# Attention's opening and end, x loaded first, and retention scores issued later

## The chip, the core and the metric

The kernel runs on one core of a Trainium2 chip. The metric is the time of one execution in microseconds (us), the median of several runs. TensorE (PE) multiplies matrices, VectorE (DVE), ScalarE (ACT) and GpSimd (POOL) do the elementwise work, and SyncE (SP) issues the DMA transfers.

## The reference

One sequence of 512 tokens, width 1024, passes through two blocks in float32. The first has a pooling mixer layer and a dilated attention layer, each followed by a convolutional feed-forward network (FFN); the conditioning vector c gives every layer a shift, a scale and a gate. The second has two layers of retention heads and stick-breaking heads side by side, each followed by a gated FFN.

```python
def _modulate(h, shift, scale): return h * (1 + scale) + shift
mod = silu(c) @ ada_w[layer] + ada_b[layer]      # sh1, sc1, g1, sh2, sc2, g2
h = _modulate(_rmsnorm(x, norm1_g), sh1, sc1)
# layer 0: y = pool_mixer(h);  layer 1:
hkv = _modulate(_rmsnorm(x, kv_norm_g), kv_shift, kv_scale)
y = dilated_attention(h, hkv @ w_kv)             # 3 branches (dilation 1, 4, 16), 16 heads of 64
x = x + g1 * y
x = x + g2 * conv_ffn(_modulate(_rmsnorm(x, norm2_g), sh2, sc2))
# second block, per layer:
ret = chunk_retention(rotary(rq), rotary(rk), rv)  # 4 heads of 128, decayed scores
sb  = stick_breaking(sq, sk, sv)                   # 4 heads of 128
x = x + concat(group_norm(ret) * silu(rg), rms_norm(sb)) @ w_out
x = x + (silu(h @ w_gate) * (h @ w_up)) @ w_down
```

## The kernel before

Activations lie transposed, features on partitions: x is eight tiles of 128x512. Every large product is made of three passes (`mm3`, L274 to L276): the weight's rounded high part times the input's high part, times the input's low part, and the weight's low part times the input's high part. So each input h is a pair of tiles, a high and a low one. Weights come as 434 units of 128x1024 (512 KB): SP loads `raw`, ACT rounds it into `wh`, and `wl = raw - wh` is made on DVE, or on POOL for every second unit while `st["spread"]` is set (L211). There are six `raw` buffers, three each of `wh` and `wl`, and eight banks of PSUM (`ps`) that PE writes.

The order of each engine's instructions is fixed when the program is built. The large products are written as plain loops, and after each `mm3` the builder adds its cost to a modelled clock (`pe["clk"]`) and calls `pump()`. That lets three streams of generators go one step further when their `ready` time has come: a generator issues some instructions and yields the microseconds until its next step. Stream 0 carries attention cores and stick-breaking heads, stream 1 norms and retention heads, stream 2 (`ada_all`) the modulation weights, a DMA of 512 KB and one DVE product (`araw`, L140 and L365) per step, `rate[0]` apart. `need(key)` runs stream 2 on at once until a modulation vector is there.

The norm before an FFN or attention is partly hidden: PE multiplies the raw x times gain by the first weights, while the statistics (`Stat`: squares on ACT, adds on POOL and for the last few on DVE, a 128x1 product on PE at L281), the reciprocal root (`rsy`) and its broadcast R follow in `norm_gen`; R and a column of shifts correct the product afterwards, and the modulated h for the rest are made one by one.

Attention runs over four head groups and, in each, three branches. `branch_qkv` makes queries, keys and values, `branch_core` is the generator of scores, softmax (`turn` transposes the exponentials at L285) and values, `combine` mixes the branches, and `out_proj` adds a head group's share of the output to x. In a retention layer `mixer2` computes for each head the query and key products, turns them with `rotary` (three DVE steps and one POOL add, L1165), and adds `ret_head` to stream 1. Nearly all DVE and ACT instructions have line L140, a helper that keeps program order.

Of the kernel before, what the change touches and what calls it, by code (L numbers as in the profile page):

```python
# [12 lines left out]
AF = mybir.ActivationFunctionType  # L13
# [3 lines left out]
P = 128  # L17
# [109 lines left out]
def model_kernel(ctx, tc, xT, wstream, adaw, vecs, crow, tab, rope, dret, selt, bandt, outT, plan, stop=None):  # L127
    order = {"on": False}

    class Kept:  # L130
# [4 lines left out]

        def __getattr__(self, name):
            f = getattr(self.engine, name)

            def call(*a, **kw):
                r = f(*a, **kw)  # L140
                return tc.keep_in_program_order(r) if order["on"] else r

            return call

# [110 lines left out]
                self.step()  # L255

    streams = [Stream() for _ in range(3)]

    def pump():
        if pe["in"]:  # L260
# [259 lines left out]
        return h, low(t, h)  # L520

    def norm_gen(stat, specs, out, residues):
        yield 2.5 if residues else 4.5
        y = rstd(stat.mean())
        yield 2.5
        out["R"] = bcast(y, residues)
        out["h"] = [[] for _ in specs]
        if not residues:
            for m in range(KT):
                out["h"][0].append(modulate(normed(out["R"], m), *specs[0], m))  # L530
            return
        xn = [normed(out["R"], m, True) for m in range(KT)]
        for hs, spec in zip(out["h"], specs):
            for m in range(KT):
                hs.append(modulate(xn[m], *spec, m))

    class RawNorm:

# [12 lines left out]
        def finish(self):  # L551
            drain(streams[1])
            return self.out["R"], self.out["h"]

    def unraw(o, R, col):
        t = S()
        nc.vector.tensor_tensor(t, o, R, op=ALU.mult)
        nc.scalar.activation(t, t, AF.Identity, bias=col)
        return t


    def pool_mixer(g1, nx):
# [14 lines left out]
        lnexp()  # L577

# [27 lines left out]
        sh.column(1)  # L606
        R = bcast(y)
        issue_low(*wh)
        us = [[ps() for _ in range(NB)] for _ in range(2)]
# [116 lines left out]

        return ap.rearrange("p (b r i) -> p b r i", b=4, r=4)

    def branch_qkv(hg, br, h, hkv, pre=()):
        d = ORDER[br]  # L730
        col = br * D + hg * 256
        qk = [("attn_w_q", (0,), 0, col), ("attn_w_q", (0,), 0, col + P),
              ("w_kv", (), 0, col), ("w_kv", (), 0, col + P)]
        vt = []
        if d == 1:

            for j in range(2):
                o = gemm([("w_kv", (), 0, 3 * D + col + j * P)], hkv, range(KT))[0]
                t = S()
                nc.scalar.activation(blocked(t), blocks(o), AF.Copy)  # L740
                vt.append(t)
        q, k = [], []
        for i in range(4):
            if i < 2 and pre:
                q.append(pre[i])
                continue
            o = gemm([qk[i]], h if i < 2 else hkv, range(KT))[0]
            t = S()
            dst, src = (t, o) if d > 1 else (blocked(t), blocks(o))
            if i < 2:  # L750
                nc.scalar.activation(dst, src, AF.Copy, scale=0.125)
                q.append(t)
            else:
                nc.vector.tensor_copy(dst, src)
                k.append(t)
        ov = [ps(), ps()]

        def part(b):
            return ov[b // 2][:, (b % 2) * 256:(b % 2) * 256 + 256]

        if d == 1:
            for b in range(NB):
                for j in range(2):
                    tr(part(b)[:, j * P:(j + 1) * P], vt[j][:, b * P:(b + 1) * P], ident)
        else:
            for kt in range(KT):
                wH, wL = wt("w_kv", (), kt * P, 3 * D + col, n=2)
                for b in range(NB):
                    xH, xL = (a[:, b * P:(b + 1) * P] for a in hkv[kt])
                    o = part(b)  # L770
                    fl = kt == 0 and b % 2 == 0
                    nc.tensor.matmul(o, xH, wH, start=fl, stop=False, skip_group_check=True)  # L772
                    nc.tensor.matmul(o, xL, wH, start=False, stop=False, skip_group_check=True)  # L773
                    nc.tensor.matmul(o, xH, wL, start=False, stop=kt == KT - 1, skip_group_check=True)  # L774
                    pe["clk"] += 0.34
                    pump()
        v = []
# [4 lines left out]
        return q, k, v  # L782

    def branch_core(hg, br, q, k, v, parts):

        d = ORDER[br]
        st4 = smp.tile([P, NB, 8], F32, tag="st4", name=nm("st4"), bufs=8)
# [85 lines left out]
            return t  # L873

        N = []
        first = scores(0)
        yield Y[0]
        first = turn(first)
        second = scores(1)
        yield Y[10]  # L880
        N.append(values(0, first))
        yield Y[11]
        second = turn(second)
# [65 lines left out]
    def attention(nx, spec, kvspec, g1, nx2):  # L949
        done = []  # L950
        parts = []
        nx.start(kvspec, spec, residues=True)
        st["spread"] = True

        outs = [("attn_w_q", (0,), 0, br * D + j * P) for br in range(2) for j in range(2)]
        pss, cols = gemm_raw(outs, nx.raw, spec[1])
        nx.raw = None
        R, (hkv, h) = nx.finish()
        pre = []
        for j, o in enumerate(pss):  # L960
# [6 lines left out]
            nc.vector.tensor_scalar(t, t, cols[:, j:j + 1], 0.125, op0=ALU.add, op1=ALU.mult)  # L967
            pre.append(t)
        nx2 = nx2()
        stat = nx2  # L970
        for hg in range(4):
            for br in range(3):
                q, k, v = branch_qkv(hg, br, h, hkv, pre[2 * br:2 * br + 2] if hg == 0 else ())
                streams[0].add(branch_core(hg, br, q, k, v, parts))
                if br == 2:
                    streams[0].add(combine(parts, done))
        out_proj(0, done, g1, stat)
        out_proj(1, done, g1, stat)
        out_proj(2, done, g1, stat)
        drain(streams[0])  # L980
        out_proj(3, done, g1, stat)
        return nx2

    def out_proj(hg, done, g1, stat):
        while len(done) <= hg:
            pe["clk"] = max(pe["clk"], streams[0].ready)
            streams[0].step()
        g1 = g1()
        for m in range(KT):
            o = gemm([("attn_w_o", (0,), 256 * hg, m * P)], done[hg], range(2))[0]  # L990
# [3 lines left out]
            if hg == 3:  # L994
                stat.add(m)
        done[hg] = None


    def head_norm(o, center):
# [106 lines left out]
    def mixer2(l, h, fin, res, dec, cosr, sinr):  # L1106
# [151 lines left out]
    nx = attention(nx, (nx.gs, mods[(1, 0)]), (gk, mods[("kv", 0)]), mod((1, 2)), next_norm("norm2_g", 1, (1, 4)))  # L1258
    if stop == 3:
        return dump()  # L1260
    need((1, 3))
# [181 lines left out]
```

## Time and profile before

| | |
|---|---|
| median of three runs | 2711.17 us (2707.82 to 2712.11) |
| the profiled execution | 2713.44 us, span 2711.7 us |
| PE busy | 2645.2 us, 98% |
| DVE, ACT, POOL busy | 52%, 38%, 12% |
| mean granted clock of PE | 0.993 |
| HBM | 109 GB/s over the span |

Times of rows count from the start of the span. "Busy" counts an engine's own instructions; idle time in front of one is put down to what released it last. PE is busy in nearly every slice, so what an edit can win is PE's idle time and the time it runs at a lower clock, and both are to be looked for by place.

### The profile page before, as it was taken

What the parts mean: (1) busy time and instruction counts of PE and PEld (TensorE: products, weight loads), DVE (VectorE), ACT (ScalarE), POOL (GpSimd) and SP (SyncE); (2) the same over time, 40 slices, a digit from 0 to 9 for tenths busy, and PEclk for the clock granted to TensorE, in tenths of its full rate; (3) what the DMA queues carried; (4) which work ended last, traced back from release to release, by engine and by line L of the source; (5) the groups of instructions that cost most, each with busy time, mean ns of one, the idle gap of its engine ahead of it and who ended that gap; (6) DMA issues with size and microseconds to landing.
All of it is one profiled execution on the core that took longest, in us unless ns stands there. A gap on an engine that the chain in (4) does not pass through costs nothing.

```text
span 2711.7 us, 32544 instructions
## 1 busy us (share of the span) xinstructions
PE 2645.2 (98%) x12952; PEld 2184.3 (81%) x12952; DVE 1399.8 (52%) x2137; ACT 1029.9 (38%) x1720; POOL 320.0 (12%) x242
## 2 busy tenths in 40 slices
PE   6999999989999999999999999999999999999998
PEld 5878888778888888788888887888888887888887
DVE  7886566764333436753444456543434347543432
ACT  4453233544434344542344451422233451422233
POOL 0000000211221212000003011210111011110111
PEclk9999999999999999999999999999999999999999
DMA  8655555443222221222323211222233221223231
GB/s 317 230 163 179 171 178 169 144 157 116 71 77 72 78 68 66 93 101 93 101 94 117 78 62 63 93 94 101 93 101 117 80 69 47 101 93 101 94 101 47
DMA packets 86230, 297.69 MB, mean 110 GB/s; under 512 B 9574, under 2 KB 10302, under 8 KB 86078
## 3 DMA queue, kind: packets, MB, share of 16 engines
q1 hardware_dynamic: 86078, 295.61, 32.6%
q8 instruction: 101, 1.65, 0.3%
q14 instruction: 51, 0.42, 0.1%
HBM read 293.48 MB, written 2.10 MB: 109 GB/s over the span
## 4 chain that ended last, share of the span: by engine, by line
PE 61%; DVE 2%; POOL 1%; issue 0%; ACT 0%; DMA 0%; SPq 0%; DVEq 0%; POOLq 0%
PE ps L274 19%; PE ps L275 18%; PE ps L276 18%; PE ps L281 4%; DVE s L140 1%; PE ps L285 1%; POOL s L1165 0%; DVE x L140 0%; DVE wl L140 0%; ACT s L140 0%; PE ps L774 0%; PE ps L773 0%; PE ps L772 0%; PE ps L1071 0%; PE ps L1070 0%
## 5 line engine op out<-in xcount | busy, mean ns | idle before, releaser
L274 PE MATMUL ps<-s,wh 128*128 128x512 f32 x3152 | 1241.4, 395 | 0.2 <-DVE s L140 0.2
L275 PE MATMUL ps<-s,wh 128*128 128x512 f32 x3152 | 1232.2, 391 | 0.0
L276 PE MATMUL ps<-s,wl 128*128 128x512 f32 x3152 | 1230.8, 391 | 0.0
L140 ACT ACTIVATE wh<-raw 128x1024 fp32r<-128x1024 f32 x434 | 459.4, 1059 | 1024.1 <-PE ps L275 783.2
L140 DVE TENSOR_TENSOR wl<-raw,wh 128x1024 fp32r<-128x1024 f32 x394 | 492.2, 1249 | 494.5 <-ACT wh L140 482.7
L274 PEld LDWEIGHTS ps<-s,wh 128*128 128x128 f32 x3152 | 593.4, 188 | 129.6 <-issue 7.2
L276 PEld LDWEIGHTS ps<-s,wl 128*128 128x128 f32 x3152 | 593.2, 188 | 125.1 <-issue 1.1
L275 PEld LDWEIGHTS ps<-s,wh 128*128 128x128 f32 x3152 | 593.8, 188 | 119.6 <-DVE s L140 0.4
L140 ACT ACTIVATE s<-s 128x512 fp32r<-128x512 f32 (+6 forms) x288 | 167.9, 584 | 182.0 <-DVE s L140 118.6
L140 DVE TENSOR_TENSOR s<-s,s 128x512 fp32r<-128x512 f32 (+3 forms) x202 | 140.4, 698 | 75.6 <-ACT s L140 74.9
L431 POOL TENSOR_TENSOR s<-s,s 128x512 f32<-128x512 f32 x40 | 62.1, 1558 | 973.0 <-ACT s L140 972.5
L140 DVE TENSOR_TENSOR s<-ps,s 128x512 f32<-128x512 f32 (+6 forms) x164 | 103.8, 647 | 139.0 <-PE ps L276 128.8
L281 PE MATMUL ps<-s,s 128*64 128x128 f32 (+7 forms) x1376 | 156.9, 309 | 16.9 <-POOL s L1165 12.6
L140 DVE TENSOR_TENSOR s<-s,ps 128x512 f32<-128x512 f32 x108 | 73.1, 686 | 194.1 <-PE ps L276 168.2
L281 PEld LDWEIGHTS ps<-s,s 128*128 128x128 f32 (+2 forms) x1376 | 124.5, 174 | 55.3 <-issue 17.9
L211 POOL TENSOR_TENSOR wl<-raw,wh 128x1024 fp32r<-128x1024 f32 x40 | 99.8, 2494 | 414.4 <-ACT wh L140 368.5
L140 ACT ACTIVATE s<-ps 128x512 f32<-128x512 f32 (+5 forms) x188 | 97.0, 530 | 114.1 <-PE ps L281 66.9
L1198 POOL TENSOR_TENSOR s<-s,s 128x512 f32<-128x512 f32 x44 | 76.4, 1737 | 536.6 <-ACT s L140 536.6
L140 DVE COPY s<-ps 128x512 f32<-128x512 f32 (+2 forms) x73 | 48.7, 673 | 148.2 <-PE ps L285 77.1
L140 DVE SCALAR_TENSOR_TENSOR araw<-araw,cond 128x1024 f32<-128x1024 f32 x96 | 119.0, 1242 | 10.4 <-DMA araw<-in_adaw 10.4
L140 ACT ACTIVATE s<-s,st 128x128 f32<-128x128 f32 (+1 forms) x192 | 79.7, 417 | 52.3 <-DVE st L140 52.3
L140 ACT ACTIVATE s<-x 128x512 f32<-128x512 f32 x72 | 45.1, 626 | 95.2 <-DVE x L140 92.7
(117 smaller groups left out, 1770.7 us busy)
## 6 DMA issues: line engine op xcount, KB each, us to landing
raw<-in_wstream SPq DMA_DIRECT2D x434, 512.0 KB, 3.3
araw<-in_adaw SPq DMA_DIRECT2D x96, 512.0 KB, 4.3
s<-in_adaw SPq DMA_DIRECT2D x32, 256.0 KB, 6.0
x<-in_xT SPq DMA_DIRECT2D x8, 256.0 KB, 5.3
s<-in_dret SPq DMA_DIRECT2D x8, 256.0 KB, 4.5
out<-s SPq DMA_DIRECT2D x8, 256.0 KB, 2.6
s<-in_rope SPq DMA_DIRECT2D x4, 256.0 KB, 5.1
cond<-in_crow SPq DMA_DIRECT2D x1, 512.0 KB, 4.0
```

The lines of the kernel that those rows point to most:

```text
L140: r = f(*a, **kw)
L211: (nc.gpsimd if u % 2 and st["spread"] else nc.vector).tensor_tensor(l, raw, h.bitcast(F32), op=ALU.subtract)
L274: nc.tensor.matmul(out, wH, xH, start=start, stop=False, **kw)
L275: nc.tensor.matmul(out, wH, xL, start=False, stop=False, **kw)
L276: nc.tensor.matmul(out, wL, xH, start=False, stop=stop, **kw)
L281: nc.tensor.matmul(out, lhsT, rhs, start=start, stop=stop, **kw)
L285: nc.tensor.transpose(out, in_, idn)
L431: eng.tensor_tensor(self.ss, self.ss, q, op=ALU.add)
L1198: nc.gpsimd.tensor_tensor(s, s, R, op=ALU.mult)
```

## The change

- **Opening.** The eight x tiles are loaded right behind the conditioning vector. The statistics' adds stand ahead of the first modulation columns, and columns are made one step ahead instead of two.
- **Norms.** `norm_gen` first waits 8.5 (was 4.5), or 4.0 (was 2.5) for attention. In attention it makes the normalised x and the modulated keys/values input tile by tile, with a yield after each, and the queries' input after them.
- **Attention's opening.** Two value and two key outputs of the first branch run k outer, so that they take the inputs in the order in which these are made; `upto` runs the norm just as far as needed. POOL makes no low parts in head group 0. The next norm's modulation (`nx2`) is asked for at the end of attention; stream 2 starts 50 later, one step each 13.
- **Cores.** For the undilated branch the transposes of values move into the core, 2.5 later. The last core starts before its values are projected, and issues both its scores first.
- **Attention's end.** Head groups 0 and 1 share one PSUM accumulation in the output product. The statistics' adds from the third on are on DVE (`last` is 6).
- **Retention.** A head's scores wait until the modelled clock is 4.0 past the end of its key product.

```diff
+    def since(clk, us):
+        return max(0.0, clk + us - pe["clk"])
...
     def norm_gen(stat, specs, out, residues):
-        yield 2.5 if residues else 4.5
+        yield 4.0 if residues else 8.5
...
-        xn = [normed(out["R"], m, True) for m in range(KT)]
-        for hs, spec in zip(out["h"], specs):
-            for m in range(KT):
-                hs.append(modulate(xn[m], *spec, m))
+        xn = []
+        for m in range(KT):
+            xn.append(normed(out["R"], m, True))
+            out["h"][0].append(modulate(xn[m], *specs[0], m))
+            yield 2.0
+        for m in range(KT):
+            out["h"][1].append(modulate(xn[m], *specs[1], m))
+            xn[m] = None
+            yield 2.5
...
+        for m in range(KT):
+            nc.sync.dma_start(x[m], xT[m])
         nc.sync.dma_start(vec, vecs)
         nc.sync.dma_start(ident, tab[:, C_ID:C_ID + P])
         for m in range(KT):
             sc.load(m)
             sh.load(m)
-            if m == 0:
-                for i in range(KT):
-                    nc.sync.dma_start(x[i], xT[i])
...
-            if m + 2 < KT:
-                columns(m + 2)
+            if m + 1 < KT:
+                columns(m + 1)
...
-        columns(0)
         for m in range(KT):
             stat.add(m)
         o = stat.mean()
-        scale_column(1)
+        scale_column(0)
...
-    def branch_core(hg, br, q, k, v, parts):
+    def branch_core(hg, br, q, k, v, vt, parts, begun, last):
...
+        if d == 1:
+            yield since(begun, 2.5)
+            ov = [ps(), ps()]
+            for b in range(NB):
+                for j in range(2):
+                    c0 = (b % 2) * 256 + j * P
+                    tr(ov[b // 2][:, c0:c0 + P], vt[j][:, b * P:(b + 1) * P], ident)
...
         first = scores(0)
+        second = scores(1) if last else None
...
     def attention(nx, spec, kvspec, g1, nx2):
...
-        st["spread"] = True
+        streams[2].ready = pe["clk"] + 50.0
+        rate[0] = 13.0
...
-        R, (hkv, h) = nx.finish()
+        nx.upto(lambda: "R" in nx.out)
+        R, (hkv, h) = nx.out["R"], nx.out["h"]
...
+        outs = [("w_kv", (), 0, 3 * D + j * P) for j in range(2)] + [("w_kv", (), 0, j * P) for j in range(2)]
+        pss = [ps() for _ in outs]
+        for kt in range(KT):
+            nx.upto(lambda: len(hkv) > kt)
+            for (name, idx, _, m0), o in zip(outs, pss):
+                wH, wL = wt(name, idx, kt * P, m0)
+                mm3(o, wH, wL, *hkv[kt], kt == 0, kt == KT - 1)
...
+        for hg in range(4):
+            st["spread"] = hg > 0
...
+        for hgs in ((0, 1), (2,), (3,)):
+            for m in range(KT):
+                o = ps()
+                for hg in hgs:
+                    part(o, m, hg, hg == hgs[0], hg == hgs[-1])
+                put(o, m)
+                if hgs[-1] == 3:
+                    nx2.add(m)
...
-    def ret_head(l, h, q, k, v, sgs, dec, out):
+    def ret_head(l, h, q, k, v, sgs, dec, out, begun):
         a = []
+        yield since(begun, 4.0)
...
-            streams[1].add(ret_head(l, hd, q, k, rv, sgs, dec, ret))
+            streams[1].add(ret_head(l, hd, q, k, rv, sgs, dec, ret, pe["clk"]))
...
-... next_norm("norm2_g", 1, (1, 4)))
+... next_norm("norm2_g", 1, (1, 4), 6))
```

The order of the program at three places. First SP's DMA queue at the start; `cond` is the conditioning vector, `vec` small parameters, `s<-in_adaw` the first modulation weights. Before:

```order
1 L175 DMA cond<-in_crow 128x1024
2 L568 DMA vec<-in_vecs 128x400
3 L569 DMA ct<-in_tab 128x128
4 L384 DMA s_91<-in_adaw 128x512
...
7 L384 DMA s_97<-in_adaw 128x512
8 L575 DMA x_74<-in_xT 128x512
...
15 L575 DMA x_81<-in_xT 128x512
```

After:

```order
1 L177 DMA cond<-in_crow 128x1024
2 L587 DMA x_74<-in_xT 128x512
...
9 L587 DMA x_81<-in_xT 128x512
10 L588 DMA vec<-in_vecs 128x400
11 L589 DMA ct<-in_tab 128x128
12 L390 DMA s_99<-in_adaw 128x512
...
15 L390 DMA s_105<-in_adaw 128x512
```

The eight x tiles have moved ahead of six other transfers.

Second, PE at attention's opening, from the product that makes the shift columns on; the `s` operands are inputs, a high and a low tile of each k step, the `ps` the outputs. Before:

```order
2152 L281 MATMUL ps_4143<-one,s_3860 128x1 x4
2153 L274 MATMUL ps_4178<-s_3941,wh_4075 128x512
2154 L275 MATMUL ps_4178<-s_3945,wh_4075 128x512
2155 L276 MATMUL ps_4178<-s_3941,wl_4077 128x512
2156 L274 MATMUL ps_4178<-s_3947,wh_4075 128x512
...
2159 L274 MATMUL ps_4178<-s_3953,wh_4075 128x512
...
2162 L274 MATMUL ps_4178<-s_3959,wh_4075 128x512
```

After:

```order
2152 L287 MATMUL ps_4065<-one,s_3860 128x1 x4
2153 L280 MATMUL ps_4085<-s_3938,wh_3971 128x512
2154 L281 MATMUL ps_4085<-s_3942,wh_3971 128x512
2155 L282 MATMUL ps_4085<-s_3938,wl_3973 128x512
2156 L280 MATMUL ps_4086<-s_3938,wh_3971 128x512
...
2159 L280 MATMUL ps_4087<-s_3938,wh_3971 128x512
...
2162 L280 MATMUL ps_4088<-s_3938,wh_3971 128x512
...
2165 L280 MATMUL ps_4085<-s_3953,wh_3971 128x512
```

Before, PE asks for a new input every three matmuls; after, every twelve.

Third, PE around the scores of the second retention head of the first such layer. `ps_12959` (before) and `ps_12858` (after) are the head's key product, the rows with 128x512, 128x384, 128x256 and 128x128 at L281 (L287) its scores, and `ps_12991` their product with the values. Before:

```order
7255 L274 MATMUL ps_12959<-s_11499,wh_12823 128x512
7256 L275 MATMUL ps_12959<-s_11500,wh_12823 128x512
7257 L276 MATMUL ps_12959<-s_11499,wl_12825 128x512
7258 L281 MATMUL ps_12969<-s_12905,s_12953 128x512
...
7261 L281 MATMUL ps_12981<-s_12905,s_12953 128x128
7262 L281 MATMUL ps_12991<-s_12662,s_12971 128x128 x2
```

After:

```order
7226 L282 MATMUL ps_12858<-s_11484,wl_12725 128x512
7227 L280 MATMUL ps_12933<-s_11115,wh_12808 128x512
...
7230 L291 MATMUL ps_12943<-ct,s_12901 128x128 x4
7231 L280 MATMUL ps_12933<-s_11166,wh_12808 128x512
...
7245 L282 MATMUL ps_12933<-s_11382,wl_12810 128x512
7246 L287 MATMUL ps_12969<-s_12852,s_12927 128x512
...
7249 L287 MATMUL ps_12981<-s_12852,s_12927 128x128
7250 L280 MATMUL ps_12933<-s_11433,wh_12808 128x512
...
7256 L287 MATMUL ps_12991<-s_12647,s_12971 128x128 x2
```

Before, the scores follow the key product at once; after, 18 matmuls of the next head's query product and four transposes stand between (7227 to 7245), and six more matmuls between scores and values.

## Rows read from the trace of the kernel before

**Rows 1.** The page: busy time, share of the span, number of instructions.

```profile
PE 2645.2 (98%) x12952; PEld 2184.3 (81%) x12952; DVE 1399.8 (52%) x2137; ACT 1029.9 (38%) x1720; POOL 320.0 (12%) x242
```

**Rows 2.** PE's waits, whole span: total us, times, longest.

```profile
PE ps L281 <- DVE s L140: 30.8, 9, 16.1
PE ps L281 <- POOL s L1165: 12.6, 8, 2.8
PE ps L285 <- ACT s L140: 7.0, 9, 2.1
```

**Rows 3.** Windows: length; PE, PEld, DVE, ACT, POOL busy; granted clock; DMA; GB/s.

```profile
480.00:500.00 20.00, 20.00 (x90) 16.57 (x89) 13.08 (x19) 8.23 (x11) 2.24 (x3) 1.00 0.36 124
...
140.00:160.00 20.00, 17.76 (x91) 14.95 (x90) 16.93 (x28) 10.85 (x15) 0.00 (x0) 1.00 0.60 190
500.00:600.00 100.00, 87.80 (x495) 70.57 (x494) 75.59 (x119) 49.49 (x91) 18.41 (x6) 0.95 0.47 158
520.00:540.00 20.00, 16.65 (x71) 13.42 (x70) 12.56 (x17) 12.69 (x18) 6.00 (x2) 0.91 0.49 158
560.00:580.00 20.00, 15.00 (x95) 10.16 (x93) 18.18 (x37) 9.23 (x30) 3.38 (x1) 0.98 0.69 236
580.00:600.00 20.00, 19.41 (x154) 17.51 (x155) 8.36 (x15) 6.78 (x15) 2.40 (x1) 0.85 0.40 133
1080.00:1100.00 20.00, 15.49 (x62) 12.51 (x61) 19.77 (x29) 11.42 (x19) 10.42 (x6) 0.86 0.12 38
1660.00:1680.00 20.00, 17.18 (x73) 13.04 (x72) 10.83 (x25) 2.11 (x4) 2.56 (x2) 0.83 0.09 27
2280.00:2300.00 20.00, 17.18 (x74) 12.92 (x73) 11.36 (x25) 1.69 (x2) 2.56 (x2) 0.83 0.08 27
```

**Rows 4.** Timeline of the opening: start, length, engine, operation, idle before and releaser.

```profile
1.25 0.42 SPq L568 DMA_DIRECT2D vec<-in_vecs  x1
...
4.08 4.85 SPq L575 DMA_DIRECT2D x<-in_xT  x8
...
5.96 1.28 ACT L140 ACT_TABLE_LOAD   x1
...
9.28 5.36 ACT L140 ACTIVATE s<-x 128x512 f32<-128x512 f32 x8 [2.04 <-DMA x<-in_xT]
...
10.61 5.47 DVE L140 TENSOR_TENSOR s<-s,s 128x512 f32<-128x512 f32 x7 [0.90 <-ACT s L140]
...
16.14 1.86 PE L281 MATMUL ps<-one,s 128*128 128x1 f32 x8 [16.14 <-DVE s L140]
...
24.96 0.80 PE L274 MATMUL ps<-wh,s 128*128 128x512 f32 x1 [3.36 <-ACT s L140]
```

**Rows 5.** Timeline of ACT, first FFN's inputs.

```profile
157.33 1.52 ACT L140 ACTIVATE s<-s,mod,gain 128x512 fp32r<-128x512 f32 x2 [1.36 <-DVE s L140]
...
160.22 1.52 ACT L140 ACTIVATE s<-s,mod,gain 128x512 fp32r<-128x512 f32 x2 [0.23 <-DVE s L140]
```

**Rows 6.** DVE: two groups of 506:580 (busy, mean ns), then its timeline near 504.

```profile
L140 DVE SCALAR_TENSOR_TENSOR araw<-araw,cond 128x1024 f32<-128x1024 f32 x10 | 13.3, 1341 | 1.8 <-DMA araw<-in_adaw 1.8
...
L140 DVE TENSOR_TENSOR wl<-raw,wh 128x1024 fp32r<-128x1024 f32 x5 | 6.1, 1223 | 0.2 <-ACT wh L140 0.2
...
504.08 0.74 DVE L140 SCALAR_TENSOR_TENSOR s<-raw,mod,s 128x512 f32<-128x512 f32 x1
...
504.86 2.88 DVE L140 SCALAR_TENSOR_TENSOR s<-raw,mod,s 128x512 f32<-128x512 f32 x1
```

**Rows 7.** PE's waits in 600:1040 (first row) and in 1040:1100.

```profile
PE ps L281 <- DVE s L140: 3.8, 3, 1.3
...
PE ps L281 <- DVE s L140: 4.5, 1, 4.5
```

**Rows 8.** Retention: PE's waits in 1600:1680, then timelines of DVE and POOL.

```profile
PE ps L281 <- POOL s L1165: 6.3, 4, 2.8
...
1665.35 2.08 DVE L140 TENSOR_TENSOR s<-ps,s 128x512 f32<-128x512 f32 x3
...
1667.57 1.26 POOL L1165 TENSOR_TENSOR s<-s,s 128x512 f32<-128x512 f32 x1 [3.83 <-DVE s L140]
```

More of the change, by code (lines that the diff above doesn't have):

```diff
@@ L553, in finish, with upto @@
             return self.out["R"], self.out["h"]
+        def upto(self, what):
+            while not what():
+                pe["clk"] = max(pe["clk"], streams[1].ready)
+                streams[1].step()
     def unraw(o, R, col):
@@ L733, in branch_qkv @@
               ("w_kv", (), 0, col), ("w_kv", (), 0, col + P)]
[L734 to L747, printed above, removed]
+        if begun is not None:
+            vt, k = begun
+        else:
+            k = []
+            vt = [values_of(gemm([("w_kv", (), 0, 3 * D + col + j * P)], hkv, range(KT))[0])
+                  for j in range(2 if d == 1 else 0)]
+        q = list(pre)
+        for i in range(len(q), 2):
+            o = gemm([qk[i]], h, range(KT))[0]
             t = S()
             dst, src = (t, o) if d > 1 else (blocked(t), blocks(o))
[L750 to L755, printed above, removed]
+            nc.scalar.activation(dst, src, AF.Copy, scale=0.125)
+            q.append(t)
+        for i in range(2 + len(k), 4):
+            k.append(keys_of(gemm([qk[i]], hkv, range(KT))[0], d))
+        v = []
+        if d == 1:
+            core(q, k, v, vt)
+            return
+        if early:
+            core(q, k, v)
         ov = [ps(), ps()]
@@ L759, in part @@
             return ov[b // 2][:, (b % 2) * 256:(b % 2) * 256 + 256]
-        if d == 1:
+        for kt in range(KT):
+            wH, wL = wt("w_kv", (), kt * P, 3 * D + col, n=2)
             for b in range(NB):
[L763 to L777, printed above, removed]
+                xH, xL = (a[:, b * P:(b + 1) * P] for a in hkv[kt])
+                o = part(b)
+                fl = kt == 0 and b % 2 == 0
+                nc.tensor.matmul(o, xH, wH, start=fl, stop=False, skip_group_check=True)
+                nc.tensor.matmul(o, xL, wH, start=False, stop=False, skip_group_check=True)
+                nc.tensor.matmul(o, xH, wL, start=False, stop=kt == KT - 1, skip_group_check=True)
+                pe["clk"] += 0.34
+                pump()
         for i in range(2):
@@ L781, in branch_qkv @@
             v.append(t)
-        return q, k, v
-    def branch_core(hg, br, q, k, v, parts):
+        if not early:
+            core(q, k, v)
+    def branch_core(hg, br, q, k, v, vt, parts, begun, last):
         d = ORDER[br]
@@ L875, in branch_core @@
         N = []
+        if d == 1:
+            yield since(begun, 2.5)
[4 more added lines that the diff above has]
+                    tr(ov[b // 2][:, c0:c0 + P], vt[j][:, b * P:(b + 1) * P], ident)
+            for o in ov:
+                t = S()
+                nc.scalar.activation(t, o, AF.Copy)
+                v.append(t)
         first = scores(0)
+        second = scores(1) if last else None
         yield Y[0]
         first = turn(first)
-        second = scores(1)
-        yield Y[10]
+        if not last:
+            second = scores(1)
+        yield 1.0 if last else Y[10]
+        while not v:
+            yield 0.5
         N.append(values(0, first))
@@ L966, in attention @@
                 nc.vector.tensor_tensor(to, perm(o, 4), r, op=ALU.mult)
-            nc.vector.tensor_scalar(t, t, cols[:, j:j + 1], 0.125, op0=ALU.add, op1=ALU.mult)
+            nc.scalar.activation(t, t, AF.Identity, scale=0.125, bias=cols[:, j:j + 1])
             pre.append(t)
-        nx2 = nx2()
[L970 to L976, printed above, removed]
@@ new lines, in attention, with core @@
+        pss = [ps() for _ in outs]
+        for kt in range(KT):
+            nx.upto(lambda: len(hkv) > kt)
+            for (name, idx, _, m0), o in zip(outs, pss):
+                wH, wL = wt(name, idx, kt * P, m0)
+                mm3(o, wH, wL, *hkv[kt], kt == 0, kt == KT - 1)
+        begun = [values_of(o) for o in pss[:2]], [keys_of(o, 1) for o in pss[2:]]
+        for hg in range(4):
+            st["spread"] = hg > 0
+            for br in range(3):
+                def core(q, k, v, vt=None):
+                    streams[0].add(branch_core(hg, br, q, k, v, vt, parts, pe["clk"], hg == 3 and br == 2))
+                    if br == 2:
+                        streams[0].add(combine(parts, done))
+                first = hg == 0 and br == 0
+                if hg == 0 and br == 2:
+                    nx.finish()
+                branch_qkv(hg, br, h, hkv, pre[2 * br:2 * br + 2] if hg == 0 else (), core, begun if first else None)
@@ L991, in out_proj, with heads, part, put @@
+        nx2 = nx2()
+        g1 = g1()
+        def heads(hg):
+            while len(done) <= hg:
+                pe["clk"] = max(pe["clk"], streams[0].ready)
+                streams[0].step()
+            return done[hg]
+        def part(o, m, hg, start, stop):
+            for kt in range(2):
+                wH, wL = wt("attn_w_o", (0,), 256 * hg + kt * P, m * P)
+                mm3(o, wH, wL, *heads(hg)[kt], start and kt == 0, stop and kt == 1)
+        def put(o, m):
             xv = x[m].rearrange("p (i r) -> p i r", r=4)
```

37 lines of the change are left out of this document (18 added, 19 removed).

## The prediction, made before the result was known

> **What bounds the kernel now.** Four views, in this order. The page's busy row [rows 1]: TensorE (PE) works 2645.2 of 2711.7 us, VectorE (DVE) half of that, so only PE's idle time (66.5 us) and the time it spends at a lower clock can be won. The change leaves the products alone: by the instruction order PE has as many large matmuls after as before. The list of waits by PE [rows 2] says for whom it idles: DVE writing an operand (30.8 us, of which 16.1 is the wait for the first statistics), GpSimd (POOL) adding rotary halves (12.6), ScalarE (ACT) writing scores that PE transposes (7.0). The windows [rows 3] say where, and what the clock did there: the granted clock stands at 1.00 in a normal stretch and is 0.83 to 0.91 in five windows just behind such waits, which means that for part of them PE was granted 1.2 instead of 2.4 GHz. Last, timelines at each place say what the late operand was itself waiting for [rows 4 to 8].
>
> I go through the six places. A loss of clock is (1 - clock) times the length of its window. A 128x512 matmul costs 0.222 us where PE is full: 90 of them in the 20 us of 480:500 [rows 3].
>
> **1. Opening.** The DMA queue issues vec at 1.25, then ct, four pieces of the first modulation weights, and only at 4.08 the first x tile; the first square waits for that tile until 9.28, 5.20 us after its issue, though ACT has been free since its table load ended at 7.24 (5.96 + 1.28). Seven adds follow on DVE, first one 1.33 us behind the first square, 5.47 us long; PE's statistics start at 16.14, its first product at 24.96 [rows 4]. After, x is issued directly behind cond, at vec's old place (1.25): the tile lands near 6.45, so the table load ends last and the squares start at 7.24, 2.04 us earlier. The adds now also stand ahead of the modulation columns on DVE, and as many columns as before (one set of two) lie between statistics and first product, so its 8.8 us stay. vec, ct and the modulation weights are late by eight issues (4.85 us); the adds (until 14.0) hide that. Gain 2.0; if x now comes in slower because it shares the first DMA burst, nothing: 0 to 2.0.
>
> **2. First FFN.** PE idles 2.24 us (20 - 17.76) in 140:160 [rows 3], waiting for the statistics' last add. The norm's first pause becomes 8.5 for 4.5, and the order puts 13 more matmuls (2.9 us) ahead: that wait goes. What is late next: the modulated inputs. ACT takes one up every 2.89 us (157.33 to 160.22) [rows 5], PE eats one per 12 matmuls, 2.67 us, and their lead is shorter now. Seven steps times 0.22 is 1.5 at most, if the lead were nil; I take half, 0.7. Gain 1.5, from 0 to 2.2.
>
> **3. Attention's opening.** In 500:600 PE idles 12.2 us (100 - 87.80), and the clock loses 1.8 (520:540), 0.4 (560:580) and 3.0 (580:600) [rows 3]: 17.4 together. The cause is DVE (18.18 of 20 busy in 560:580): ten modulation-weight products of 1.34 us (13.3) fall in 506 to 580 because a later norm's scale is demanded at once, and POOL's low parts stretch its steps: the form that takes 0.74 at 504.08 takes 2.88 at 504.86 [rows 6]. Keys and values then come one output at a time, each demanding all eight modulated inputs at the start. After: the demand moves to attention's end, the weight products come one per 13 us of the modelled clock starting 50 later (32 x 13 + 50 = 466 us, attention lasts some 570), POOL makes no low parts in the first head group, and two values and two keys outputs run k outer, so that PE wants a new input only every 12 matmuls while DVE's share of one is two ops of about 0.7 plus half a low part of 1.22, 2.0 and under 2.67. Cost of the cover gone: the six low parts that POOL makes in 500:600 are 6 x 1.22 = 7.3 us more on DVE, which is 75.59 busy there and loses the 13.3 [rows 3, 6]. First late thing left: the first transposes of exponentials, two waits near 1, and transposed values now sitting in the core (0.6): I leave 2.6. Gain 17.4 - 2.6 = 14.8; low 9.0 (5.4 of waits left and 3.0 of the clock), high 17.4.
>
> The clock needs a word. In 520:540 (3.4 us idle) and behind waits of 4.5 and 2.8 us it fell [rows 3, 7, 8]; but in 580:600 it fell as well, where the waits before were ACT's nine, the longest 2.1 [rows 2]. The Trainium skill (TensorE: Matmul & The Clock Gate, Why this matters for your kernels) asks only that no long idle gap stand between bursts of matmuls. By that the short waits I leave would cost no clock and the sum stays; by the row at 580:600 several short ones can cost another 3, which is rival A.
>
> **4. Head groups 1 to 3.** Three waits, 3.8 us [rows 7], the longest 1.3, where scores of the undilated branch need keys that DVE has just copied. Eight transposes of values and some matmuls (12 more instructions in the order, over 2 us) now stand between. Gain 3.8; if the transposes wait for ACT's copy instead, 1.5.
>
> **5. Attention's end.** 4.5 us of waiting for statistics [rows 7] and 0.14 x 20 = 2.8 of clock: 7.3. DVE is 19.77 of 20 busy in 1080:1100 [rows 3]. After: two head groups' output products share one accumulation (8 steps go from DVE), six adds of about 0.7 (2.08 for three such steps [rows 8]) come to it from POOL, and 54 more matmuls (12 us) stand ahead of the statistics, the next FFN's first outputs. So the add has 12 us where it was 4.5 late. The last core starts before its values are projected and both its scores go first. New: waits for the last values' copy and the norm's result, which I estimate at 0.7 + 0.9 = 1.6, each a part of the 1.3 that a wait for such a copy cost at a head group's start [rows 7]. Gain 5.7 (3 to 7.3).
>
> **6. Retention, two layers.** Each layer waits 6.3 us in four heads for POOL's rotary add [rows 8], and its clock loses 0.17 x 20 = 3.4 [rows 3]. At the worst head the three DVE steps took 2.08 and POOL's add 1.26 [rows 8]. After, 18 to 24 matmuls (4.0 to 5.3 us) of the next product stand between a head's keys and its scores, instead of none: the chain of 3.34 fits unless DVE has a low part in front (1.22 [rows 6]), which leaves about 0.65 (3.34 + 1.22 - 4.0 = 0.56, and a little for the hand-overs) in two heads of the four. Gain per layer 9.7 - 1.3 = 8.4, for two 16.8; low 8 (half, if the scores' products with the decay become the wait), high 19.4.
>
> **Sum.** 2.0 + 1.5 + 14.8 + 3.8 + 5.7 + 16.8 = 44.6. The profiled execution took 2713.4 us (its span 2711.7 and 1.7 around it), so 2668.8; it is 2.2 over the median of the runs, 2711.2, so I forecast 2666.6. The ends of the terms give 2.0 + 2.2 + 17.4 + 3.8 + 7.3 + 19.4 = 52.1, or 2659, and 0 + 0 + 9 + 1.5 + 3 + 8 = 21.5, or 2690.
>
> **Rivals.** A: the clock falls as before. Short waits remain at each place, and PE at 580 was slowed after short ones. For: that window. Against: most of the waits ahead of it go. Price 5.2 + 2.8 + 6.8 = 14.8, so 2681.
> B: waits move on. Later scores make the values, the head's norm and the output projection late; inputs one at a time starve PE. If half of the idle time that I count as won (44.6 - 14.8 = 29.8) comes back, and with it the clock: 2666.6 + 14.9 + 14.8 = 2696. For: DVE is close to full behind each of these waits. Against: the order shows other matmuls between at every place.
> C, slower: DVE saturates in the first head group. It takes over POOL's low parts and still carries weight products; each of the six turns of scores and their transposes in three cores would wait behind one of each (1.22 + 1.34, times 18 is 46), and each core would pay the clock once more (3 x 3.4 = 10): 56, so 2723. It decides once DVE has no idle time in windows between 580 and 700. Against: 8.36 of 20 in 580:600.
> D: the edits don't reach the engines' order. The order of the changed kernel excludes it, except that DMA may still set the opening: 2711 stays for want of anything better.
>
> **Chances.** Forecast 0.68, A 0.15, B 0.09, C 0.06, D 0.02. The forecast's own range is 2658 to 2680. From 2657 to 2695 are held the forecast, A and about half of B: 0.85, less some for a gain beyond the ends. Within 0.2% (5 us) is what a measurement of this kernel can't tell from no change. Faster 0.68 + 0.15 + 0.08; same D and the last 0.01 of B; slower C.
>
> **What would show it.** First statistics near 14.1 and first product near 23. In 140:160 PE at 20 or close. No wait over 1.5 between the first branch's query products and 580, clock 1.00 up to 600, and DVE's weight products spread through all of attention. Waits for POOL's rotary add down from 12.6 to under 4. The wait of 4.5 at attention's end gone. PE idle near 37 (66.5 - 29.8) instead of 66.5. I am wrong if a new wait over 2 us stands in the list, if the clock still shows 0.83 at the fourth retention head, or if DVE is full in the first head group.

## The result, and the profile after

The changed kernel takes 2668.83 us (median of four runs, 2668.51 to 2669.09); the kernel before, measured again beside it, 2710.68 (2707.82 to 2712.11). The ratio is 0.9847, with a 95% interval of 0.983 to 0.9864: 42 us faster, where 44.6 were forecast (2666.6). The profiled execution took 2668.51, its span is 2666.8, 44.9 shorter than before.

The page's busy row after, against [rows 1]:

```profile
PE 2630.5 (99%) x12952; PEld 2178.0 (82%) x12952; DVE 1393.0 (52%) x2139; ACT 1031.4 (39%) x1724; POOL 293.9 (11%) x229
```

PE idles 36.3 us of its span (66.5 before), and is busy 14.7 us less with the same 12952 products: the first is waits that went (30.2), the second nearly all the clock (13.0 in the table below). Its waits after, against [rows 2] (total us, times, longest; ACT, DVE and POOL lines have their own numbers now):

```profile
PE ps L287 <- DVE s L142: 14.1, 1, 14.1
PE ps L287 <- POOL s L1229: 3.6, 4, 1.4
PE ps L280 <- ACT s L142: 3.4, 1, 3.4
PE ps L287 <- DVE rsy L471: 2.7, 2, 1.8
PE ps L287 <- DVE rsy L142: 1.5, 1, 1.5
PE ps L291 <- ACT s L747: 0.9, 1, 0.9
PE ps L291 <- DVE cc L961: 0.5, 1, 0.5
PE ps L287 <- DVE s L437: 0.4, 1, 0.4
PE ps L976 <- DVE s L969: 0.3, 1, 0.3
```

The waits for scores to be transposed (7.0) are 0.9, those for POOL's rotary add (12.6) are 3.6, and apart from the opening's 14.1 and the last statistics' 0.4 DVE's 30.8 are gone. New is `rsy`, the reciprocal root, in both FFN norms; the kernel before had that wait at attention's norm:

```profile
507.87 1.16 PE L281 MATMUL ps<-ct,rsy 128*128 128x128 f32 x8 [1.27 <-DVE rsy L140]
```

Windows after, against [rows 3]:

```profile
140.00:160.00 20.00, 18.19 (x85) 15.03 (x84) 15.09 (x25) 9.09 (x13) 0.00 (x0) 0.91 0.53 168
500.00:600.00 100.00, 98.76 (x602) 81.46 (x603) 68.19 (x103) 62.66 (x133) 0.00 (x0) 1.00 0.32 106
560.00:580.00 20.00, 19.91 (x175) 18.21 (x171) 10.00 (x18) 9.02 (x24) 0.00 (x0) 1.00 0.37 121
1060.00:1080.00 20.00, 19.07 (x93) 15.78 (x92) 18.62 (x32) 8.68 (x14) 0.00 (x0) 1.00 0.28 86
1600.00:1620.00 20.00, 18.59 (x92) 14.69 (x90) 15.30 (x34) 4.85 (x7) 3.64 (x3) 1.00 0.24 79
```

500:600 has 1.24 us of idle time for 12.2 and the full clock for 0.95. One window is worse: 140:160 now stands at 0.91, where it was at 1.00. The opening, against [rows 4]:

```profile
1.25 4.13 SPq L587 DMA_DIRECT2D x<-in_xT  x8
...
7.42 4.27 ACT L142 ACTIVATE s<-x 128x512 f32<-128x512 f32 x8
...
8.61 5.47 DVE L142 TENSOR_TENSOR s<-s,s 128x512 f32<-128x512 f32 x7 [7.67 <-ACT s L142]
...
14.13 1.87 PE L287 MATMUL ps<-one,s 128*128 128x1 f32 x8 [14.13 <-DVE s L142]
...
22.96 0.80 PE L280 MATMUL ps<-wh,s 128*128 128x512 f32 x1 [3.37 <-ACT s L142]
```

The squares start right behind the table load, which ends at 7.41, and everything follows 2.0 us earlier, to the first product at 22.96.

By place, the span's 44.9 us divide so (idle time from the waits and windows, clock as (1 - clock) times the window):

| place | forecast | measured |
|---|---|---|
| opening | 2.0 | 2.0 |
| first FFN | 1.5 | 2.2 - 1.8 - 1.8 (clock) = -1.4 |
| attention's opening | 14.8 | 12.2 - 1.2 + 5.2 = 16.2 |
| head groups 1 to 3 | 3.8 | 3.8 - 0.5 (a new wait for `cc`) = 3.3 |
| attention's end | 5.7 | 4.5 + 2.8 + (0.8 + 0.4, not counted) - 0.9 - 0.3 = 7.3 |
| retention | 16.8 | 12.6 - 3.6 + 6.8 = 15.8 |
| sum | 44.6 | 43.2, and 1.7 outside these rows |

Of the 1.7, 0.7 is the clock of 1100:1110, behind the windows that the prediction took: 0.93 before, 1.00 after. The rest is not placed.

### The profile page after: what moved, and what is told of

It reads as the page before. It is cut to its first block, busy times and chain, and to the rows that moved or that the text cites. A ratio compares the mean times of both kernels' runs of the same rounds, so it can differ in the third digit from the quotient of the medians.

```text
span 2666.8 us, 32530 instructions
## 1 busy us (share of the span) xinstructions
PE 2630.5 (99%) x12952; PEld 2178.0 (82%) x12952; DVE 1393.0 (52%) x2139; ACT 1031.4 (39%) x1724; POOL 293.9 (11%) x229
## 4 chain that ended last, share of the span: by engine, by line
PE 92%; DVE 4%; ACT 1%; DMA 1%; issue 1%; POOL 0%; SPq 0%; DVEq 0%; ACTq 0%; POOLq 0%
PE ps L280 27%; PE ps L282 27%; PE ps L281 27%; PE ps L287 6%; PE ps L291 1%; PE ps L796 1%; PE ps L798 1%; PE ps L797 1%; DMA araw<-in_adaw 1%; DVE araw L373 1%; DVE wl L213 0%; DVE s L437 0%; DVE s L355 0%; DVE s L336 0%; ACT s L516 0%
## 5 line engine op out<-in xcount | busy, mean ns | idle before, releaser
L281 PE MATMUL ps<-s,wh 128*128 128x512 f32 x3152 | 1229.0, 390 | 0.0
L208 ACT ACTIVATE wh<-raw 128x1024 fp32r<-128x1024 f32 x426 | 450.8, 1059 | 1012.3 <-PE ps L281 771.3
L281 PEld LDWEIGHTS ps<-s,wh 128*128 128x128 f32 x3152 | 592.5, 188 | 118.4
L287 PE MATMUL ps<-s,s 128*64 128x128 f32 (+7 forms) x1376 | 150.6, 302 | 3.8 <-POOL s L1229 3.6
L287 PEld LDWEIGHTS ps<-s,s 128*128 128x128 f32 (+2 forms) x1376 | 120.9, 171 | 38.7 <-issue 15.6
L213 POOL TENSOR_TENSOR wl<-raw,wh 128x1024 fp32r<-128x1024 f32 x31 | 75.5, 2437 | 421.5 <-ACT wh L208 399.4
L1264 DVE TENSOR_TENSOR s<-s,ps 128x512 f32<-128x512 f32 x44 | 30.3, 688 | 140.6 <-PE ps L282 128.1
L456 ACT ACTIVATE s<-s 128x512 f32<-128x512 f32 x96 | 59.6, 624 | 101.7 <-DVE s L718 85.5
L351 ACT ACTIVATE s<-s 128x512 fp32r<-128x512 f32 x104 | 65.5, 630 | 70.9 <-POOL s L983 42.8
L352 DVE TENSOR_TENSOR s<-s,s 128x512 fp32r<-128x512 f32 x104 | 71.4, 687 | 30.6 <-ACT s L351 30.5
L1259 DVE TENSOR_TENSOR s<-ps,s 128x512 f32<-128x512 f32 x44 | 30.4, 691 | 106.3 <-PE ps L282 106.3
L280 PE MATMUL ps<-wh,s 128*128 128x512 f32 x192 | 77.6, 404 | 3.4 <-ACT s L142 3.4
L281 PE MATMUL ps<-wl,s 128*128 128x512 f32 x192 | 75.9, 395 | 0.0
```

The lines of the kernel that those rows point to most:

```text
L208: nc.scalar.activation(h, raw, AF.Copy)
L213: (nc.gpsimd if u % 2 and st["spread"] else nc.vector).tensor_tensor(l, raw, h.bitcast(F32), op=ALU.subtract)
L280: nc.tensor.matmul(out, wH, xH, start=start, stop=False, **kw)
L281: nc.tensor.matmul(out, wH, xL, start=False, stop=False, **kw)
L287: nc.tensor.matmul(out, lhsT, rhs, start=start, stop=stop, **kw)
L351: nc.scalar.activation(h, src, AF.Copy)
```

## The experiments

Twelve kernels. Unless said otherwise each is the changed kernel with one edit, and is set against its 2668.8; the kernel before, run beside each, had medians of 2710.0 to 2711.4. Runs of one edited kernel differ by up to 8 us here (of the kernel before by 11), those of the changed one by only 0.6, so differences of two or three between medians settle nothing by themselves; then the profile's rows decide. One place moves whatever the edit is: in the ten profiles whose program is the changed kernel's up to the first FFN, PE idles there between 1.3 and 2.8 us, and the clock in 140:160 is 1.00 in three of them and 0.91 in seven.

**Retention scores at once.**

```diff
     def ret_head(l, h, q, k, v, sgs, dec, out, begun):
         a = []
-        yield since(begun, 4.0)
```

> The changed kernel, but retention scores are issued at once behind the key product again (no pause of 4.0). Theory (the waits for POOL's rotary add and the clock they cost are what that part won): per layer the wait goes from 1.8 back to 6.3 us and the clock loses 3.4 again, so 2 x 7.9 = 15.8 us more than 2668.8, 2684.6. Rival (the clock loss hung on other waits that are gone now): only the idle time comes back, 9 us, 2677.8.

Measured 2680.81 (2679.33 to 2682.27), ratio to before 0.9892 (0.9877 to 0.9907): 12.0 more, between the theory's 15.8 and the rival's 9. Its wait for POOL over the span, and the windows behind the fourth heads of the two layers:

```profile
PE ps L287 <- POOL s L1228: 12.5, 8, 2.8
```

```profile
1640.00:1660.00 20.00, 18.32 (x91) 15.13 (x92) 9.13 (x26) 4.22 (x6) 1.26 (x1) 1.00 0.18 59
2260.00:2280.00 20.00, 20.00 (x92) 16.18 (x93) 9.17 (x26) 4.23 (x6) 0.00 (x0) 0.91 0.15 53
```

All eight waits are back, to a tenth (12.5 for 12.6, longest 2.8). The clock is not: 1.00 and 0.91 where the kernel before has 0.83 twice [rows 3]. So the pause is what removed the waits; that the clock fell behind them before was a likely companion, not a fixed price.

**The pause alone, in the kernel before.** The same pause added to the kernel before: `since`, the yield, and the clock at the end of the key product handed to `ret_head`.

> The kernel before, with only the pause of 4.0 ahead of retention scores. Theory (the part stands by itself; the waits go from 12.6 to 3.6 and the clock's two losses of 3.4 at the fourth heads go with them): 15.8 less than 2710.7, 2694.9. Rival (the clock's losses there were chance, as they were mostly missing when the pause was taken out of the changed kernel): the idle time alone, 9 less, 2701.7, or between the two.

Measured 2699.79 (2694.7 to 2703.19), ratio 0.9959 (0.9946 to 0.9971): 11.6 less than the 2711.4 beside it. The part stands by itself, and its worth is the same 12 from either side, with 9.0 of it idle time: the waits for POOL are 3.6, four of them, longest 1.4, as in the changed kernel. In its profile the clock is full at the place too, and another place is worse:

```profile
1660.00:1680.00 20.00, 19.96 (x100) 16.14 (x100) 13.65 (x33) 4.85 (x7) 2.24 (x1) 1.00 0.15 53
```

```profile
140.00:160.00 20.00, 17.03 (x76) 14.22 (x77) 16.28 (x28) 8.84 (x13) 0.00 (x0) 0.91 0.60 186
```

With 1.00 in 2260:2300 as well, the theory's 15.8 are all there; at the first FFN, which the edit doesn't touch, the wait is 3.4 for 2.2 and the clock 0.91 for 1.00, which takes 3.0 back.

**A longer pause there.** `yield since(begun, 5.5)` for 4.0.

> The changed kernel, with the pause before retention scores 5.5 instead of 4.0. Theory (what is left are waits for POOL's add in two heads a layer, 0.4 and 1.4): both go, 2 x 1.8 = 3.6 less, 2665.2. Rival (the decayed scores, the values' product or the head's output become late instead): no gain, 2668 to 2672.

Measured 2662.35 (2660.38 to 2664.94), ratio 0.9826 (0.981 to 0.9842): 6.5 less. No wait for POOL is left, and nothing behind the scores became late; the theory's 3.6 are in it. The rest is not all accounted for; 1.8 of it may be the clock, which stayed at 1.00 in 140:160 in its profile.

**The first FFN's pause taken back** (4.5 for the first norm, 8.5 for the second).

> The changed kernel, but the first FFN's norm pauses 4.5 before its statistics as in the kernel before (the second FFN's keeps 8.5). Theory (at this place the longer pause only moved the wait from the statistics to the reciprocal root and let the clock fall): the wait of 2.2 for the statistics returns, the wait of 1.8 and the 1.8 of clock go, so 1.4 less, 2667.4. Rival (the clock falls behind whichever wait stands there): 0.4 more than 2668.8, 2669.2 or above.

Measured 2672.48 (2668.18 to 2672.87), ratio 0.9858 (0.9842 to 0.9874): 3.7 more, the rival's side. The wait that came back is not 2.2 but 3.5, and the clock is at 0.83 behind it:

```profile
142.53 1.87 PE L287 MATMUL ps<-one,s 128*128 128x1 f32 x8 [3.55 <-DVE s L437]
```

So by the medians the longer pause is worth having there too; in the profiles it replaces 3.5 by 1.8. The size is that of one execution: DVE's last step on x ahead of this place is at 139.92 in it, late among the ten profiles (137.08 to 139.93), and one of its four runs, 2668.18, lost nothing.

**x loaded late again.** The eight transfers go back behind the first four modulation pieces.

> The changed kernel, but x is loaded behind vec, the transpose matrix and the first four modulation pieces again. Theory (up to the first FFN DVE sets the pace, with modulation products that wait for their DMA, so the 2.0 that PE gains at the opening it waits at the first FFN, where the wait moved from 2.2 to 3.6 when only the pause was taken back): PE comes 2.0 later and waits 1.8 less there, and the clock does not fall: 2665 to 2669, not above 2668.8. Rival (the opening's gain is kept to the end): 2.0 more, 2670.8.

Measured 2671.06 (2668.22 to 2672.49), ratio 0.9854 (0.984 to 0.9867): 2.2 more by the medians, which is the rival's number, but within the spread of its runs. In its profiled execution (2668.22) the first product is at 25.05, 2.1 later, and the wait at the first FFN is 0.8 instead of 1.8: half of what the opening gains is waited for again there. With the clock, 1.00 in 140:160 for 0.91, nothing of it is left in this pair of executions. DVE's last step on x ahead of the first FFN, first in the changed kernel, then here:

```profile
137.74 0.76 DVE L675 SCALAR_TENSOR_TENSOR x<-ps,mod,x 128x512 f32<-128x512 f32 x1
```

```profile
138.70 0.75 DVE L676 SCALAR_TENSOR_TENSOR x<-ps,mod,x 128x512 f32<-128x512 f32 x1
```

DVE is 1.0 later where PE is 2.1 later, and the step moves more than that without an edit ahead of it: the range of the ten profiles is 2.9 wide. Up to there DVE is nearly full (90.80 of 100 us in 40:140 of the changed kernel) and works through modulation products that wait for their DMA (waits of DVE in 30:142 of the changed kernel):

```profile
DVE araw L373 <- DMA araw<-in_adaw: 7.1, 8, 1.7
```

How much of the 2.0 reaches the end is not settled by these runs: all of it by the medians, none in the profile.

**The broadcast later.** `yield 2.5 if residues else 4.5` ahead of the FFN norms' broadcast.

> The changed kernel, with the broadcast of the reciprocal root 4.5 instead of 2.5 behind the statistics in the FFN norms. Theory (PE waits there only because DVE reaches the root's four small steps late): 1.8 and 1.8 of clock go at the first FFN, 0.9 at the second, so 4.5 less, 2664.3. Rival (the modulated inputs that follow the broadcast are then late by the same time): the wait moves on, 2668.8 or up to 2 more.

Measured 2669.31 (2667.97 to 2669.77). The edit tells nothing of the theory: no engine's order changed, the broadcast stood at the same place already. The run shows how well a median repeats, 0.5 us apart.

**Modulation demanded at attention's start**, in the old pace.

```diff
-        streams[2].ready = pe["clk"] + 50.0
-        rate[0] = 13.0
...
+        nx2 = nx2()
         for hg in range(4):
...
-        nx2 = nx2()
```

> The changed kernel, but the next norm's modulation is demanded at attention's start again and the weight products keep the old pace (6.0, no start 50 later). Theory (DVE, loaded with 16 weight products of 1.3 us, is what made the first turns wait): 20 us of DVE work stand ahead of the first scores, so PE waits 6 to 10 us and the clock falls once (3.4): 2678 to 2682. Rival (the order of the inputs, k outer, is what counts and DVE has room): within 1.5 of 2668.8.

Measured 2673.02 (2672.9 to 2676.54), ratio 0.9866 (0.9851 to 0.9881): 4.2 more, under half of what the theory named. PE's waits in 500:640 of its profile:

```profile
PE ps L291 <- ACT s L747: 4.3, 1, 4.3
PE ps L281 <- DVE s L521: 0.7, 1, 0.7
PE ps L291 <- ACT s L853: 0.4, 1, 0.4
PE ps L280 <- ACT s L515: 0.2, 1, 0.2
```

The weight products make the inputs late, and most is paid at one place, where the first values are to be transposed. These waits are 4.7 more than the changed kernel's 0.9, and the clock is 0.91 in 540:560: 6.5 at this place. The total is less because the first FFN, ahead of the edit, has a wait of 1.3 for 1.8 and a clock of 1.00 for 0.91 in this execution.

**One output at a time** in the first branch, all eight inputs first.

```diff
-        pss = [ps() for _ in outs]
-        for kt in range(KT):
-            nx.upto(lambda: len(hkv) > kt)
...
+        nx.upto(lambda: len(hkv) == KT)
+        pss = [gemm([o], hkv, range(KT))[0] for o in outs]
```

> The changed kernel, but the two value and two key outputs of the first branch come one at a time, each over all eight inputs, instead of k outer. Theory (an output at a time takes an input every 0.7 us while DVE and ACT make one every 2.2 or more): PE waits 4 to 9 us for the last inputs and the clock falls once (3.4): 2676 to 2681. Rival (the inputs have lead enough, the weight products' pace was the cure): within 1.5 of 2668.8.

Measured 2674.69 (2674.12 to 2676.13), ratio 0.987 (0.9855 to 0.9885): 5.9 more, just under the theory's range. The first two of its waits in 500:640:

```profile
PE ps L291 <- ACT s L747: 2.8, 1, 2.8
PE ps L291 <- ACT s L853: 0.8, 1, 0.8
```

The others are one of 0.5 for a weight's low part and four for single inputs, 0.7 together; the clock stays at 1.00 in 540:560, so 3.9 of the 5.9 are seen as waits and the theory's fall of the clock did not come. Most of attention's 16.2 stays when either of the two parts is taken away, so neither is the cause alone. Both away at once was not run, and neither were the other edits at this place: the norm's longer pause, the inputs made tile by tile, and four steps on the queries that ACT does now (L1009) and DVE did before (L967), which the list of the change leaves out.

**POOL helps in head group 0** (`st["spread"] = True`).

> The changed kernel, but POOL makes every second low part of the weights in head group 0 too. Theory (a low part on POOL holds up DVE's steps by some 2 us, and in this stretch these are waited for): 2 to 5 more, 2671 to 2674. Rival (with the weight products gone DVE has room for it): within 1 of 2668.8.

Measured 2668.79 (2667.09 to 2669.2), ratio 0.9846 (0.9832 to 0.9861): the rival's side, no difference. Once the weight products had gone, taking POOL out of that group bought nothing from 558 on, where the first low part on POOL stands in this run's profile. The four that the kernel before has between 504 and 547, while the inputs are made, do not come back with this edit, so what their absence is worth is not shown.

**The second FFN's pause taken back** (8.5 for the first norm, 4.5 for the second).

> The changed kernel, but the second FFN's norm pauses 4.5 before its statistics as in the kernel before (the first FFN's keeps 8.5). Theory (the pause of 54 matmuls is what took the wait of 4.5 away): 4 to 5 of the wait come back and 2.8 of clock, less the 0.9 for the reciprocal root: 2674 to 2676. Rival (the merged output product and the adds on DVE had already done it): within 1 of 2668.8.

Measured 2672.71 (2669.31 to 2673.74), ratio 0.9858 (0.9842 to 0.9875): 3.9 more, below the theory's range. A wait of 1.5 for the statistics comes back, not 4.5, and 0.09 of the clock in 1060:1080 (1.8); with the root's 0.9, which goes, that is 2.4 of the 3.9. The rest of the old wait stays away without the longer pause, so the other edits at this place took it; which of them is not shown.

**Attention's end in the old form, with the pause kept.** Four separate output products and the adds on POOL again.

```diff
-        for hgs in ((0, 1), (2,), (3,)):
+        for hgs in ((0,), (1,), (2,), (3,)):
...
-... next_norm("norm2_g", 1, (1, 4), 6))
+... next_norm("norm2_g", 1, (1, 4)))
```

> The changed kernel, but the four head groups' output products are added to x one by one again and the statistics' adds but two are on POOL (attention's end in the old form, with the pause of 54 matmuls kept). Theory (the pause alone has some 10 us to spare, and took the wait away): within 1 of 2668.8. Rival (DVE, 19.8 of 20 busy there, falls behind by its 8 further steps and POOL's slowing): the root of the statistics comes 3 to 5 later, and with the clock 2672 to 2677.

Measured 2675.21 (2669.83 to 2677.62), ratio 0.9873 (0.9858 to 0.9888): 6.4 more by the medians, the rival's range. In its profile, an execution of 2669.83, the old wait of 4.5 stays away; what grew are others, three of the list over the whole span (2.7, 0.5 and 0.3 in the changed kernel):

```profile
PE ps L287 <- DVE rsy L471: 3.4, 2, 2.0
...
PE ps L291 <- DVE cc L961: 1.7, 2, 1.2
...
PE ps L976 <- DVE s L969: 1.4, 1, 1.4
```

The root at the second FFN is waited for 2.0, 1.1 more and not 3 to 5, and the clock is full there; this fastest of its executions, 1.0 above 2668.8, is at the edge of what the theory allows. What made the three others 4 to 8 slower has no profile.

**A better version.** Pauses of 5.5 ahead of the retention scores and 4.0 (for 2.5) ahead of the undilated values' transposes.

> The changed kernel with the pause before retention scores 5.5 and the one before the transposes of undilated values 4.0 (was 2.5; six matmuls later in PE's order). Theory (the waits left by the changed kernel each want a little more work ahead): 3.6 from retention and the 0.9 of the first transposes less, 2664.3 at most; with what the run with 5.5 alone showed, 2661 to 2662. Rival (the scores behind the transposes are then late for the softmax): 2662.4 to 2665.

Measured 2661.8 (2660.19 to 2663.46), ratio to before 0.9821 (0.9807 to 0.9834): the fastest here, all its runs under all of the changed kernel's. Its waits:

```profile
PE ps L287 <- DVE s L142: 14.3, 1, 14.3
PE ps L280 <- ACT s L142: 3.4, 1, 3.4
PE ps L287 <- DVE rsy L471: 2.9, 2, 2.0
PE ps L287 <- DVE rsy L142: 1.5, 1, 1.5
PE ps L291 <- DVE cc L961: 0.5, 1, 0.5
PE ps L287 <- DVE s L437: 0.4, 1, 0.4
PE ps L976 <- DVE s L969: 0.3, 1, 0.3
```

The waits for POOL and for the first transposes are gone, and none took their place. Against the 5.5 alone (2662.35) it is not to be told apart. What is left is the opening (19.2) and the root in the two norms.

## Why the prediction was right, and the step of it that failed

The mechanism held: the products are untouched, six families of waits and the clock losses behind them were what could be won, and other work was put in front of most of them. The forecast came within 2.3 us. That it came so near is luck in part: against the table the first FFN is 2.9 short, retention 1.0 and the head groups 0.5, attention's opening and end are 1.4 and 1.6 over, and 1.7 was in no term. Of the signs named beforehand one failed, PE close to 20 in 140:160 (18.19).

**The opening** came out as worked out, to a tenth; that part of it would be waited for again at the first FFN was not in the sum.

**The first FFN is the step that failed.** I wrote "that wait goes" and then looked for what is late next among the modulated inputs. What is late next is the reciprocal root, one step sooner; the wait of 1.27 for it at attention's norm could have told it. DVE after, at that place:

```profile
144.26 0.15 DVE L477 TENSOR_SCALAR var<-ps 128x4 f32<-128x4 f32 x1
144.38 1.54 DVE L336 SCALAR_TENSOR_TENSOR s<-raw,mod,s 128x512 f32<-128x512 f32 x2
145.84 0.15 DVE L467 TENSOR_TENSOR rsb<-rsy 128x4 f32<-128x4 f32 x1
145.91 1.22 DVE L213 TENSOR_TENSOR wl<-raw,wh 128x1024 fp32r<-128x1024 f32 x1
...
148.56 0.16 DVE L471 TENSOR_TENSOR rsy<-rsy,rsb 128x4 f32<-128x4 f32 x1
```

The root's steps take 0.15 each, but shift sums of 0.75 and a low part of 1.22 lie between them, so the chain needs 4.5 us from `var` to `rsy`, and `var` itself starts 2.7 behind the end of the statistics' product (141.59), as DVE has other steps in front of it. PE, which no longer waits in front of the statistics, reaches the broadcast 1.8 before the root is there, and then runs at 1.2 GHz for a while:

```profile
148.78 1.38 PE L287 MATMUL ps<-ct,rsy 128*128 128x128 f32 x8 [1.81 <-DVE rsy L471]
...
150.38 0.63 PE L280 MATMUL ps<-s,wh 128*128 128x512 f32 x1
```

Such a matmul is recorded with 0.39 ahead of the wait. So 1.5 forecast became -1.4. The wait for the root is there in all ten profiles, the fall of the clock in seven. The run with the pause taken back (3.7 more by the medians, wait 3.5) says that the pause itself was right; DVE's lateness, not PE's order, sets this place.

**Attention's opening** was under-sized by 1.4: I left 2.6 of waits, 1.2 remained. That its cause was DVE's load and the order of the inputs is borne out in halves: 4.2 comes back without the paced weights (6.5 at the place itself), 5.9 without k outer. POOL's absence, which I counted among the causes, was worth nothing from 558 on; ahead of that, where its low part stretched DVE's step, it was not tested.

**Head groups, attention's end.** The three waits went, as forecast (a new one of 0.5 for the combine came); no run takes the moved transposes back, so that they did it is read from the order alone. The end gave 7.3 for 5.7, since the combine's waits, which I had left out, shrank too. I credited the pause with that wait, and counted 54 more matmuls, 12 us, ahead of the statistics. The order has 45 behind the last output product, where it had 24: 21 more, 4.7 us, hardly more than the wait. In the profile after, the last add ends at 1069.2 and PE takes the statistics up at 1071.75: 2.5 to spare. So the pause and DVE's relief share the wait, as the two runs on this place say.

**Retention** gave 15.8 for 16.8: I left 0.65 in two heads a layer and found 0.4 and 1.4. The idle time was the certain part (9.0). The clock's 6.8 were right for this pair of profiles, but a price that is not paid each time: the same waits cost 0 and 1.8 of clock in the profile of the run that put them back.

**Rivals.** A did not come: the clock is full at all places but the first FFN. There, behind one wait of 1.8, it fell (0.91), and it stayed full behind one of the two waits of 2.8 in the run that puts the retention waits back. The rule quoted beside the sum (The Trainium skill, TensorE: Matmul & The Clock Gate, Why this matters for your kernels), no long idle gap between bursts of matmuls, would not have led one to expect the fall behind 1.8; the rows decide. B came at one place, the first FFN. C did not: DVE is 10.00 of 20 busy in 560:580, and 63.50 of 120 in the stretch that was to decide it:

```profile
580.00:700.00 120.00, 119.49 (x755) 97.82 (x754) 63.50 (x108) 53.23 (x144) 18.24 (x10) 1.00 0.34 111
```

D is excluded by the rows.

## What to carry to other kernels

When a wait is taken away by giving the waiting engine other work, follow the chain behind it step by step on the engine that was late, small steps in their queue included: the next one may be as late by nearly as much. Price idle time from the waits as certain and the clock behind them as a chance. And what an engine gains by starting earlier can be waited for again where a fuller engine beside it comes in; look for where the two meet before counting it.

## What was unexpected of the hardware

The clock does not fall by the length of a wait alone. It fell to half behind one of 1.8 us (0.91 in 140:160 after) but not behind one of 2.2 at the same place before [rows 3], and the same retention waits of 2.8 us went with 0.83 in one kernel and with 1.00 or 0.91 in another. At the first FFN seven profiles of one program up to there have a wait of 2.0 for the root; the clock stands at 0.91 in six of them and at 1.00 in the seventh, that of the longer pause ahead of retention scores. What decides it is open; it was not tried.
